# A hybrid decoder layer on one core: the scan's state update moved ahead of its decay products, and the last products cut at 512, 384 and 128 tokens

## The chip, the cores and the metric

The kernel runs on one core of one Trainium2 chip. A core has five engines with a queue of their own each: PE (TensorE, matrix products; its weight loads are listed apart as PEld), DVE (VectorE), ACT (ScalarE), POOL (GpSimd) and SP (SyncE, which here issues most of the transfers). The metric is the device time of one execution in microseconds (us).

## The reference

One layer of a decoder over 1040 positions (16 meta tokens and 1024 real ones) of width 1024. After a norm and one input projection, three groups of heads work side by side: stick-breaking attention, a Mamba-2 state-space scan, and latent attention (MLA). Their outputs go through one projection and are added; then come a norm, a SwiGLU feed-forward layer of width 2816, and a last norm over the features of each token. All is float32. The scan, in blocks of 128 tokens, is what the first edit touches:

```python
seg = Acs[:, :, :, None] - Acs[:, :, None, :]
Ldec = jnp.exp(jnp.where(tri[None, None, :, :, None, None], seg, -jnp.inf))
CB = jnp.einsum('bclgn,bcsgn->bclsg', Cc, Bc)
y_diag = jnp.einsum('bclsgj,bcsgjp->bclgjp', CB[..., None] * Ldec, X)
...
states = jnp.einsum('bclgn,bclgjp->bcgjpn', Bc, X * decay[..., None])
...
def step(carry, inp):
    cd, st = inp
    return carry * cd[..., None, None] + st, carry
...
y_off = jnp.einsum('bclgn,bcgjpn->bclgjp', Cc, prev) * jnp.exp(Acs)[..., None]
return (y_diag + y_off).reshape(b, L, H, P)
```

The second edit touches the end: `h + (silu(fn @ w_gate) * (fn @ w_up)) @ w_down`, then `rmsnorm(h, final_norm_g)`.

## The kernel before

Features lie on the 128 partitions and tokens along the rows, so a product takes a 128x128 piece of a weight as its stationary operand and up to 512 tokens as its moving one. For accuracy each float32 operand is split into a high and a low part, and each product is done as three (high by high, low by high, high by low), which accumulate in one bank of PSUM.

The order of instructions is not written out by hand. The code gives a program order with priorities, and a scheduler with a timeline of its own places each engine's instructions; an engine then runs its own list strictly in that order. So a moved line of code can move many instructions, also of neighbouring stages.

**The scan** (`ssd_chunk`, L764 to L856) runs over nine chunks c (the first holds the 16 meta tokens) and, within a chunk, over two groups g of eight heads; one pair (c, g) is called a half-step here. In a half-step:

- L802: products R spread the running sums of the decay over all partitions, four heads to a bank; ACT makes from them `cd` (the chunk's decay), `ea` (the decay since the chunk's start, one buffer, L811) and, head by head, the exponents of the decay matrices L (L814), then L itself (L824). DVE makes `dec` (L805).
- L820: POOL makes Xd, the inputs times the decay to the chunk's end.
- L826 to L829: product cbp; DVE masks it and multiplies it into L.
- L834, L835: product yo of the state S[g] with C; DVE multiplies it into `ea`.
- L838: eight products yd of the inputs X with L.
- L843, L844: POOL adds `ea` to the output y, then DVE adds yd to it.
- L847 to L854 (not in the last chunk): product sps, POOL multiplies S[g] by cd (L851), DVE adds sps to it (L854). The next chunk's yo of the same g reads S[g].

yo, yd and sps take their banks in turn from one pool of two buffers (`yps`, tag "y"); R has two of its own. While the scan runs, PE also works on dense projections whose rows are L147 to L149 (`dense_fm`: high by high, low by high, high by low): they fill PE between the scan's products.

**The end** (L1600 to L1689). The last products, of the first four of the 22 feed-forward blocks, are done by parts of the tokens. `last_part(t0, n)` does, for each of the eight output blocks o, `down` (12 products of n columns, L1618 to L1620, and DVE's add into the residual hF, L1122), then a square by ACT (L1640). In the first two parts the squares are added up by POOL and DVE, and `token_rstd` sums them over the partitions (L158, one product for each 128 tokens), scales (L169) and takes the power -1/2 on POOL (L170). In the last part (`by_pe`) PE sums each square directly (L1633, one product for each 128 tokens and each o, three blocks late), then DVE scales (L1656) and POOL takes the power (L1657). `last_row` spreads the result over the partitions (L176, one product for each 128 tokens), and `last_norm` copies that row (L1671) and multiplies: some blocks by ACT and POOL (L1676, L1677), the others by DVE (L1679); SP sends each ng finished blocks out (L1681). The row of a part is spread and its norm done while the next part's products run.

```python
r0, _ = last_part(0, 512)
r1, row = last_part(512, 256, between=r0)
last_norm(0, 512, row, (3, 6), 2)
r2, row = last_part(768, 256, True, r1)
last_norm(512, 256, row, range(0, KT, 2), 4)
last_norm(768, 256, last_row(*r2), (1, 4), 2)
```

Of the kernel before, what the change touches and what calls it, by code (L numbers as in the profile page):

```python
# [11 lines left out]
F32 = mybir.dt.float32  # L12
# [47 lines left out]
def tile_hybrid_block(ctx: ExitStack, tc: tile.TileContext, a: dict):  # L60
# [689 lines left out]
    with ExitStack() as st:  # L750
# [13 lines left out]
        def ssd_chunk(c):  # L764
# [26 lines left out]
            for g in range(2):  # L791
# [31 lines left out]
                if c > 0:  # L823
                    act.activation(L, L, AF.Exp, scale=-1.0)  # L824
                    pcb = tp.tile([128, 512], F32, tag="tp", name="cbp")
                    pe.matmul(pcb[:, :128], bc[:, g, :], bc[:, 2 + g, :], start=True, stop=True)  # L826
                    cbm = p2.tile([128, 128], F32, tag="cbm", name="cbm")
                    dve.tensor_tensor(cbm, pcb[:, :128], tri, op=ALU.mult)
                    dve.tensor_tensor(L, L, cbm.unsqueeze(1).to_broadcast([128, 8, 128]), op=ALU.mult)  # L829
                    yo = yps.tile([128, 512], F32, tag="y", name="yo")  # L830
                    yd = yps.tile([128, 512], F32, tag="y", name="yd")
                    for j in range(4):
                        ts = slice(128 * j, 128 * (j + 1))
                        pe.matmul(yo[:, ts], S[g][:, ts], bc[:, 2 + g, :], start=True, stop=True)  # L834
                    dve.tensor_tensor(ea, ea, yo.rearrange("p (j t) -> p j t", j=4), op=ALU.mult)  # L835
                    for h in range(8):
                        hh = 8 * g + h
                        pe.matmul(  # L838
                            yd[64 * (h % 2) : 64 * (h % 2) + 64, 128 * (h // 2) : 128 * (h // 2 + 1)],
                            X[:, hh * 64 : (hh + 1) * 64], L[:, h, :], start=True, stop=True,  # L840
                        )
                    yg = y[:, 4 * g : 4 * g + 4]
                    pool.tensor_tensor(yg, yg, ea, op=ALU.add)  # L843
                    dve.tensor_tensor(yg, yg, yd.rearrange("p (j t) -> p j t", j=4), op=ALU.add)  # L844
                if c < 8:
                    sps = yps.tile([128, 512], F32, tag="y", name="sps")
                    pe.matmul(sps, btok[:n, g * 128 : (g + 1) * 128], Xd[:n, gs], start=True, stop=True)  # L847
                    if c == 0:
                        dve.tensor_copy(S[g], sps)
                    else:  # L850
                        pool.tensor_tensor(  # L851
                            heads(S[g]), heads(S[g]), cd.unsqueeze(2).to_broadcast([128, 8, 64]), op=ALU.mult
                        )
                        dve.tensor_tensor(S[g], S[g], sps, op=ALU.add)  # L854
            if c > 0:
                act.dma_start(s_y[:, :, 128 * (c - 1) : 128 * c].rearrange("j p t -> p j t"), y)  # L856

# [765 lines left out]
    def last_part(t0, n, by_pe=False, between=None):  # L1623

        ts = slice(t0, t0 + n)
        blocks = [(128 * b, 128) for b in range(n // 128)]
        squares, sums = [], []

        def column_sums(o):
            if o == 0:  # L1630
                sums.extend(ffn_bank() for _ in blocks)
            for (b0, w), ps in zip(blocks, sums):
                pe.matmul(ps[:, 0:1], squares[o][:, b0 : b0 + w], ones[:, 0:1], start=(o == 0), stop=(o == KT - 1))  # L1633

        for o in range(KT):
            down(o, t0, n)
            if o == 2 and between:
                row = last_row(*between)
            sq = q_tile("tt")[:, :n]
            act.activation(sq, hT[o][:, ts], AF.Square)  # L1640
            if by_pe:
                squares.append(sq)
                if o >= 3:
                    column_sums(o - 3)
            elif o == 0:
                squares.append(sq)
            else:
                add(squares[0], squares[0], sq, dve if o >= 5 else pool)
        if by_pe:
            for o in range(KT - 3, KT):  # L1650
                column_sums(o)
        with tc.high_priority(offset=1000):
            if sums:
                r = ga.tile([128, len(blocks)], F32, tag="rl", name="rl")
                for e, ps in enumerate(sums):
                    dve.tensor_scalar(r[:, e : e + 1], ps[:, 0:1], 1.0 / D, EPS, ALU.mult, ALU.add)  # L1656
                pool.tensor_tensor(r, r, mhalf[:, : len(blocks)], op=ALU.pow)  # L1657
            else:
                r = token_rstd(ga, bank(), squares, blocks, D)
        return (r, blocks), row if between else None  # L1660
# [21 lines left out]

    rstds = wa.tile([128, 1024], F32, tag="wraw", bufs=1, name="rstds")
    r0, _ = last_part(0, 512)
    r1, row = last_part(512, 256, between=r0)
    last_norm(0, 512, row, (3, 6), 2)
    r2, row = last_part(768, 256, True, r1)
    last_norm(512, 256, row, range(0, KT, 2), 4)
    last_norm(768, 256, last_row(*r2), (1, 4), 2)  # L1689


def _units(w, width=128):
# [85 lines left out]
```

## Time and profile before

| | |
|---|---|
| three timed runs | 1761.19, 1754.87, 1760.85 us (median 1760.85) |
| the profiled execution | 1762.44 us, of which its span is 1760.7 |
| mean granted TensorE clock | 0.986 |
| busy PE / DVE / ACT / POOL | 1706.4 / 1140.2 / 846.2 / 720.0 us |
| moved by DMA | 222.35 MB |

The span runs from the first to the last instruction of the profiled execution. A row of the timeline gives start and length in us, the engine, the line of the code, the operation, output and inputs by the program's names, the shape, how many equal rows are merged (x8), and in brackets the idle time before it with what ended it. A float32 product that is not split is recorded as two rows, so the 8 products yd of a half-step are 16 records. A group's row gives the count, the busy total in us and the mean length of one in ns, then the idle time before them. A row of waits gives who waited for whom, the total in us, the times and the longest. PE's rows overlap: the pace of a stream is the distance from start to start.

### The profile page before, as it was taken

To read this page: it belongs to the slowest core of one execution; us is meant where nothing else is said; L and a number is where in the kernel's file an instruction comes from. 1 tells how busy PE (TensorE), PEld (TensorE's weight loads), DVE (VectorE), ACT (ScalarE), POOL (GpSimd) and SP (SyncE) were. 2 spreads that over 40 slices of the span, in tenths; PEclk is the share of its full clock that TensorE was granted. 3 is DMA by queue.
4 is the path that set the end of the run, shared out by engine and by line. 5 is a ranking of instruction groups with operands and counts; after the bars stand their busy time and mean duration, and the time that the engine had idled before them with its cause. 6 is when DMAs were issued, how large, how long until landed. Compare 5 with 4: busy or idle time off the path is not lost. (4 is left out here: it accounts for less than half of the span.)

```text
span 1760.7 us, 26573 instructions
## 1 busy us (share of the span) xinstructions
PE 1706.4 (97%) x9801; PEld 1500.3 (85%) x9801; DVE 1140.2 (65%) x1742; ACT 846.2 (48%) x1797; POOL 720.0 (41%) x498
## 2 busy tenths in 40 slices
PE   8979999999999899999999999999999999999998
PEld 7969989999987788998888888778888888878887
DVE  7778666678444663555575655986566666688644
ACT  7546565655467646675454425432222232244332
POOL 3334346344466657563321346544455545200012
PEclk9989999999999999999999998999999999999998
DMA  4312232122533645347330443123333223999702
GB/s 162 82 56 64 71 86 79 58 71 73 156 111 115 200 157 154 108 125 244 110 91 29 124 155 102 60 84 101 109 102 102 96 90 104 314 370 386 254 1 97
DMA packets 145639, 222.35 MB, mean 126 GB/s; under 512 B 24722, under 2 KB 84148, under 8 KB 145508
## 3 DMA queue, kind: packets, MB, share of 16 engines
q1 hardware_dynamic: 126112, 205.09, 35.9%
q10 hardware_dynamic: 19396, 15.56, 2.9%
q8 instruction: 77, 1.26, 0.3%
q14 instruction: 54, 0.44, 0.1%
HBM read 157.56 MB, written 63.04 MB: 125 GB/s over the span
## 5 line engine op out<-in xcount | busy, mean ns | idle before, releaser
L147 PE MATMUL d_ps<-hnh,whi 128*128 128x384 f32 (+6 forms) x744 | 250.1, 336 | 7.4 <-DVE KS L610 4.7
L149 PE MATMUL d_ps<-hnl,whi 128*128 128x384 f32 (+6 forms) x744 | 246.7, 332 | 0.0
L148 PE MATMUL d_ps<-hnh,wlo 128*128 128x384 f32 (+6 forms) x744 | 245.8, 330 | 0.0
L136 POOL TENSOR_TENSOR wlo<-wraw,whi 128x1024 fp32r<-128x1024 f32 (+1 forms) x57 | 138.0, 2420 | 222.7 <-ACT whi L134 218.3
L147 PEld LDWEIGHTS d_ps<-hnh,whi 128*128 128x128 f32 (+1 forms) x744 | 141.0, 190 | 12.5 <-issue 6.1
L148 PEld LDWEIGHTS d_ps<-hnh,wlo 128*128 128x128 f32 (+1 forms) x744 | 141.2, 190 | 2.8 <-issue 0.5
L149 PEld LDWEIGHTS d_ps<-hnl,whi 128*128 128x128 f32 (+1 forms) x744 | 140.9, 189 | 2.8 <-issue 0.2
L1285 PE MATMUL b_ps<-T,wl 128*128 128x512 f32 x352 | 138.8, 394 | 1.3 <-POOL wl L1116 1.3
L1286 PE MATMUL b_ps<-T,wh 128*128 128x512 f32 x352 | 138.2, 394 | 1.3 <-DVE T L1116 1.3
L1284 PE MATMUL b_ps<-T,wh 128*128 128x512 f32 x352 | 139.1, 396 | 0.0
L315 DVE TENSOR_TENSOR pl<-ptg,ph 128x512 fp32r<-128x512 f32 (+1 forms) x160 | 99.3, 627 | 48.2 <-ACT ph L314 46.9
L1115 ACT CAST op<-raw 128x1024 fp32r<-128x1024 f32 x69 | 71.3, 1050 | 107.4 <-PE d_ps L1570 59.2
L1116 DVE TENSOR_TENSOR op<-raw,op 128x1024 fp32r<-128x1024 f32 x69 | 84.8, 1239 | 39.0 <-ACT op L1115 38.9
L704 DVE TENSOR_TENSOR_SCAN cm<-cm,zcol 128x144 f32<-128x144 f32 (+3 forms) x64 | 101.7, 1593 | 12.3 <-ACT cm L702 11.9
L314 ACT CAST ph<-ptg 128x512 fp32r<-128x512 f32 (+1 forms) x160 | 85.2, 543 | 39.9 <-PE ptg L331 24.7
L1116 POOL TENSOR_TENSOR wlo<-raw,whi 128x1024 fp32r<-128x1024 f32 x18 | 45.6, 2531 | 110.0 <-ACT whi L1115 110.0
L1116 POOL TENSOR_TENSOR wl<-raw,wh 128x512 fp32r<-128x512 f32 x46 | 74.4, 1625 | 29.2 <-ACT wh L1115 29.2
L1115 ACT CAST wh<-raw 128x512 fp32r<-128x512 f32 x88 | 53.1, 615 | 67.2 <-PE b_ps L1286 67.1
L1122 POOL TENSOR_TENSOR tt<-tt 128x512 f32<-128x512 f32 (+1 forms) x8 | 8.1, 1011 | 186.1 <-ACT tt L1640 185.9
L1012 ACT ACTIVATE pr<-sc_ps,sm 128x256 f32<-128x256 f32 (+4 forms) x112 | 59.8, 540 | 46.8 <-DVE sm L1009 24.8
L1285 PEld LDWEIGHTS b_ps<-T,wl 128*128 128x128 f32 x352 | 66.5, 189 | 16.8 <-POOL wl L1116 1.6
L502 DVE SCALAR_TENSOR_TENSOR cacc<-d_ps,cw,cacc 128x384 f32<-128x384 f32 (+3 forms) x108 | 61.7, 571 | 29.5 <-ACT cacc L495 27.4
(442 smaller groups left out, 5180.8 us busy)
## 6 DMA issues: line engine op xcount, KB each, us to landing
raw<-in_w_down_dram SPq DMA_DIRECT2D x99, 256.0 KB, 5.3
s_hops<-gs SPq DMA_DIRECT2D x63, 256.0 KB, 2.0
raw<-s_hops SPq DMA_DIRECT2D x63, 256.0 KB, 5.4
raw<-in_w_gate_dram SPq DMA_DIRECT2D x22, 512.0 KB, 3.6
raw<-in_w_up_dram SPq DMA_DIRECT2D x22, 512.0 KB, 4.1
wraw<-in_w_o_dram SPq DMA_DIRECT2D x16, 512.0 KB, 4.5
wraw<-in_w_xbc_dram SPq DMA_DIRECT2D x12, 512.0 KB, 3.6
s_xs<-csig SPq DMA_DIRECT2D x24, 192.0 KB, 1.9
```

What stands on the lines that cost most here:

```text
L136: pool.tensor_tensor(lo[:, :cols], raw[:, :cols], f32(hi[:, :cols]), op=ALU.subtract)
L147: pe.matmul(ps[:m, :n], wh, mh, start=(kt == 0), stop=False)
L148: pe.matmul(ps[:m, :n], wl, mh, start=False, stop=False)
L149: pe.matmul(ps[:m, :n], wh, ml, start=False, stop=(kt == nkt - 1))
L314: act.copy(ph[:, :n], pt[:, :n])
L315: dve.tensor_tensor(pl[:, :n], pt[:, :n], f32(ph[:, :n]), op=ALU.subtract)
L704: dve.tensor_tensor_scan(rev, rev, zcol.to_broadcast([128, n_all]), 1.0, ALU.mult, ALU.add)
L1115: act.copy(hi, value)
L1116: eng.tensor_tensor(lo, value, f32(hi), op=ALU.subtract)
L1284: pe.matmul(banks[j], hi[:, ks], UH[u][k], start=start and k == 0, stop=False, skip_group_check=skip)
L1285: pe.matmul(banks[j], lo[:, ks], UH[u][k], start=False, stop=False, skip_group_check=skip)
L1286: pe.matmul(banks[j], hi[:, ks], UL[u][k], start=False, stop=stop and k == 3, skip_group_check=skip)
```

## The change

In a half-step, the state's update (sps, POOL's multiply, DVE's add) stands in the program ahead of the yd products and the two additions to y; yd takes its bank behind sps, no longer behind yo. At the end the parts are 512, 384 and 128 tokens long, no longer 512, 256 and 256; the middle part's outputs go out by two blocks at a time, no longer by four.

```diff
                     yo = yps.tile([128, 512], F32, tag="y", name="yo")
-                    yd = yps.tile([128, 512], F32, tag="y", name="yd")
                     for j in range(4):
...
                     dve.tensor_tensor(ea, ea, yo.rearrange("p (j t) -> p j t", j=4), op=ALU.mult)
-                    for h in range(8):
-                        hh = 8 * g + h
-                        pe.matmul(
-                            yd[64 * (h % 2) : 64 * (h % 2) + 64, 128 * (h // 2) : 128 * (h // 2 + 1)],
-                            X[:, hh * 64 : (hh + 1) * 64], L[:, h, :], start=True, stop=True,
-                        )
-                    yg = y[:, 4 * g : 4 * g + 4]
-                    pool.tensor_tensor(yg, yg, ea, op=ALU.add)
-                    dve.tensor_tensor(yg, yg, yd.rearrange("p (j t) -> p j t", j=4), op=ALU.add)
                 if c < 8:
                     sps = yps.tile([128, 512], F32, tag="y", name="sps")
...
                         dve.tensor_tensor(S[g], S[g], sps, op=ALU.add)
+                if c > 0:
+                    yd = yps.tile([128, 512], F32, tag="y", name="yd")
+                    for h in range(8):
...
+                    yg = y[:, 4 * g : 4 * g + 4]
+                    pool.tensor_tensor(yg, yg, ea, op=ALU.add)
+                    dve.tensor_tensor(yg, yg, yd.rearrange("p (j t) -> p j t", j=4), op=ALU.add)
...
-    r1, row = last_part(512, 256, between=r0)
+    r1, row = last_part(512, 384, between=r0)
     last_norm(0, 512, row, (3, 6), 2)
-    r2, row = last_part(768, 256, True, r1)
-    last_norm(512, 256, row, range(0, KT, 2), 4)
-    last_norm(768, 256, last_row(*r2), (1, 4), 2)
+    r2, row = last_part(896, 128, True, r1)
+    last_norm(512, 384, row, range(0, KT, 2), 2)
+    last_norm(896, 128, last_row(*r2), (1, 4), 2)
```

What the scheduler makes of the first edit is seen on PE around the ninth half-step with yd. Before (xtp and btp are transposes, rows L147 to L149 the dense products between):

```order
L781 MATMUL xtp<-identr,xs 128x128 x4
L789 MATMUL btp<-identr,bc 128x128 x2
L838 MATMUL yd<-L,X 64x128 x8
L847 MATMUL sps<-Xd,btok 128x512
L147 MATMUL d_ps<-lhi,whi 128x272
```

Now (line numbers are one or more higher or lower; sps is L837, yd L849, and the dense rows here are those of the values, L916 to L918):

```order
L918 MATMUL d_ps<-wlo,lhi 128x512
L837 MATMUL sps<-Xd,btok 128x512
L781 MATMUL xtp<-identr,xs 128x128 x4
L789 MATMUL btp<-identr,bc 128x128 x2
L849 MATMUL yd<-L,X 64x128 x8
L916 MATMUL d_ps<-whi,lhi 128x512
```

sps has moved from behind yd to ahead of it, with transposes between, and other dense products surround the half-step. On DVE, in the scan's first third, the additions to the state (S_5503 is group 0's) and to y stood so before:

```order
L844 TENSOR_TENSOR y<-y,yd 128x512
L854 TENSOR_TENSOR S_5503<-S_5503,sps 128x512
L828 TENSOR_TENSOR cbm<-cbp,tri 128x128
L829 TENSOR_TENSOR L<-L,cbm 128x1024
L835 TENSOR_TENSOR ea<-ea,yo 128x512
```

and stand so now (L844 is the addition to the state, L855 that to y, L834 the product into ea):

```order
L844 TENSOR_TENSOR S_5503<-S_5503,sps 128x512
L805 TENSOR_TENSOR dec<-R,AT 128x4
L855 TENSOR_TENSOR y<-y,yd 128x512
L834 TENSOR_TENSOR ea<-ea,yo 128x512
L828 TENSOR_TENSOR cbm<-cbp,tri 128x128
L829 TENSOR_TENSOR L<-L,cbm 128x1024
```

The state's addition has moved ahead of y's, and here the product into ea ahead of that into L. At the end of POOL's list (the hF numbers are the eight output blocks, 15847 to 15854) before:

```order
L170 TENSOR_TENSOR rc<-rc,mhalf 128x2
L1677 TENSOR_TENSOR outt<-hF_15847,rstds 128x256
L1677 TENSOR_TENSOR outt<-hF_15849,rstds 128x256
L1677 TENSOR_TENSOR outt<-hF_15851,rstds 128x256
L1677 TENSOR_TENSOR outt<-hF_15853,rstds 128x256
L1657 TENSOR_TENSOR rl<-rl,mhalf 128x2
L1677 TENSOR_TENSOR outt<-hF_15848,rstds 128x256
L1677 TENSOR_TENSOR outt<-hF_15851,rstds 128x256
```

Now:

```order
L170 TENSOR_TENSOR rc<-rc,mhalf 128x3
L1678 TENSOR_TENSOR outt<-hF_15847,rstds 128x384
L1678 TENSOR_TENSOR outt<-hF_15849,rstds 128x384
L1678 TENSOR_TENSOR outt<-hF_15851,rstds 128x384
L1678 TENSOR_TENSOR outt<-hF_15853,rstds 128x384
L1658 TENSOR_TENSOR rl<-rl,mhalf 128x1
L1678 TENSOR_TENSOR outt<-hF_15848,rstds 128x128
L1678 TENSOR_TENSOR outt<-hF_15851,rstds 128x128
```

The order of the steps is the same; the four norms of the middle part ahead of the last power are wider, what follows it is narrower. All line numbers below are those of the kernel before, unless said otherwise.

More of the change, by code (lines that the diff above doesn't have):

```diff
@@ L854, in ssd_chunk @@
                         dve.tensor_tensor(S[g], S[g], sps, op=ALU.add)
+                if c > 0:
+                    yd = yps.tile([128, 512], F32, tag="y", name="yd")
+                    for h in range(8):
+                        hh = 8 * g + h
+                        pe.matmul(
+                            yd[64 * (h % 2) : 64 * (h % 2) + 64, 128 * (h // 2) : 128 * (h // 2 + 1)],
+                            X[:, hh * 64 : (hh + 1) * 64], L[:, h, :], start=True, stop=True,
+                        )
+                    yg = y[:, 4 * g : 4 * g + 4]
+                    pool.tensor_tensor(yg, yg, ea, op=ALU.add)
+                    dve.tensor_tensor(yg, yg, yd.rearrange("p (j t) -> p j t", j=4), op=ALU.add)
             if c > 0:
```

## The prediction

> **What bounds the kernel now.** I read the page first, then the busy times by stage, then the waits of the scan (the stage of the state-space chunks), then the timeline of the end.
>
> ```profile
> span 1760.7 us, 26573 instructions
> PE 1706.4 (97%) x9801; PEld 1500.3 (85%) x9801; DVE 1140.2 (65%) x1742; ACT 846.2 (48%) x1797; POOL 720.0 (41%) x498
> ```
>
> PE is busy for 1706.4 of 1760.7 us, so all its idle time together is 54.3 us. The stages say where it lies (columns: length, busy of PE, PEld, DVE, ACT, POOL, granted clock, DMA share, GB/s):
>
> ```profile
> 470.00:650.00 180.00, 170.21 (x1233) 143.47 (x1233) 103.53 (x173) 112.26 (x314) 108.74 (x74) 0.98 0.48 150
> 650.00:1100.00 450.00, 440.13 (x2606) 395.59 (x2606) 248.07 (x489) 240.16 (x550) 196.01 (x129) 0.98 0.42 127
> 1722.00:1760.70 38.70, 30.57 (x254) 30.11 (x253) 17.32 (x41) 11.17 (x26) 12.09 (x15) 0.89 0.31 110
> ```
>
> The scan lies in the first row: PE idles 9.8 us there. The last row holds the two parts of 256 tokens; PE is full until the chain after its last product. So the first edit can win at most what PE idles in the scan, and the second acts on PE's own time and on the chain behind it. The idle of the scan, in its two bad places:
>
> ```profile
> 540.00:550.00 10.00, 7.47 (x50) 6.46 (x51) 4.23 (x6) 7.86 (x24) 7.35 (x6) 0.68 0.26 81
> 580.00:620.00 40.00, 34.21 (x256) 28.14 (x254) 28.52 (x45) 24.53 (x68) 24.65 (x16) 1.00 0.60 198
> ```
>
> In the first the granted clock also falls to 0.68. Who waits for whom there (total us, times, longest):
>
> ```profile
> ACT ea L811 <- POOL y L843: 22.3, 9, 4.0
> DVE L L829 <- ACT L L824: 19.6, 12, 4.2
> ...
> PE yd L838 <- DVE L L829: 4.7, 8, 1.2
> ...
> PE R L802 <- ACT L L814: 2.3, 4, 1.4
> ...
> DVE S L854 <- POOL S L851: 1.5, 1, 1.5
> ...
> PE yo L834 <- DVE y L844: 1.4, 1, 1.4
> ```
>
> PE waits at yd for the decay matrices, at R for ACT to empty a bank, and once at yo for the output sum. No row has PE waiting for the state itself. ACT loses 22.3 us at ea, whose only buffer POOL's sum has to release.
>
> **The sum's base.** The profiled execution took 1762.44 us, its span and 1.74 us around it; that is 1.59 us above the median of the runs shown, 1760.85. I add changes to 1762.44 and carry them over to the median.
>
> **Part one, the state's update ahead of yd.** The update is one product (sps), POOL's multiply and DVE's add, with no DMA; the instructions stay the same and their order changes. yo, yd and sps share two PSUM buffers in turn. Before, the next half-step's yo takes the buffer of yd, and so waits for L844 behind the whole L chain: the 1.4 us row. Now it takes that of sps, which L854 empties earlier. That 1.4 us goes. Late next is sps, which takes yd's buffer of the half-step before; it stands a half-step later, so L844 is long done. On DVE L854 now stands ahead of L844 and at times of L829; while it waits (for POOL: 1.5 us once), L829 and with it yd wait behind it.
>
> The waits at yd and R (4.7 and 2.3 us) would shrink only if the L chain came earlier against PE's queue. It might: ACT's L exponentials stand behind ea, and with yo no longer behind L844, ea, POOL's sum and the next ea may come earlier in each half-step. But PE's order was rebuilt with the same belief. By the order, 112 dense products stood between the scan's last yd and the first MLA scores; now it is 184. Thus 72 products have left the scan as cover. At 384 columns,
>
> ```profile
> 651.67 0.34 PE L149 MATMUL d_ps<-hnl,whi 128*128 128x384 f32 x1
> ...
> 654.84 0.34 PE L149 MATMUL d_ps<-hnl,whi 128*128 128x384 f32 x1
> ```
>
> (18 products in 3.17 us, 0.1761 us each), that is 72 x 0.1761 = 12.7 us by which the scan must run faster, or PE idles more. The bounds of part one: -9.8 us (all idle gone), +12.7 us (the cover gone, the pace as it was). I take the 1.4 us that has a mechanism, and 0.5 us (a tenth) of the 4.7: -1.9 us. The reordered rows up to the MLA attention have 9.9 us of idle (second stage row) and no wait that the edit names; I leave them at zero.
>
> **Part two, 512, 384 and 128 tokens.** Each part has 8 x 4 x 3 = 96 products. At 256 columns:
>
> ```profile
> 1722.27 0.28 PE L1618 MATMUL b_ps<-op 128*128 128x256 f32 x1
> ...
> 1727.13 0.27 PE L1620 MATMUL b_ps<-op 128*128 128x256 f32 x1
> ```
>
> 41 steps in 4.86 us, 0.1185 us each; at 384 it is 0.1761. For 128 columns no such stream exists. The nearest rows:
>
> ```profile
> 68.50 0.27 PE L697 MATMUL sc_ps<-KS,Q 128*128 128x144 f32 x1
> ...
> 68.61 0.27 PE L700 MATMUL sc_ps<-sb_mask,identr 128*128 128x128 f32 x1
> ...
> 68.72 0.34 PE L696 MATMUL sc_ps<-K,Q 128*128 128x272 f32 x1
> ```
>
> ```profile
> 636.40 1.09 PE L838 MATMUL yd<-L,X 128*64 128x128 f32 x16
> ```
>
> ```profile
> 1749.38 1.88 PEld L1633 LDWEIGHTS b_ps<-ones,tt 128*128 128x128 f32 x16
> ```
>
> With a load of 128 columns for each, short products follow one another at 0.11 us (68.50, 68.61, 68.72), and bare loads at (1.88 - 0.19) / 15 = 0.113. With loads of 64 columns 128-column products follow at (1.09 - 0.27) / 15 = 0.055. So the weight load, not the columns, sets the pace: 0.11 us, between 0.055 and 0.1185. [...]
>
> PE until its last product: 96 x (0.1761 + 0.11) = 27.5 us against 192 x 0.1185 = 22.8: +4.7. Small products among them: 20 before (sums 4 + 2, spreads 4 + 2, column sums 8), now 18 (4 + 3, 4 + 3, 4), each two records of 0.113: -0.45. So PE's last product ends 4.3 us later. Behind it, before:
>
> ```profile
> 1746.70 0.61 PE L176 MATMUL d_ps<-identr,rc 128*128 128x128 f32 x4
> ...
> 1747.79 2.81 POOL L1677 TENSOR_TENSOR outt<-hF,rstds 128x256 f32<-128x256 f32 x4 [3.33 <-ACT rstds L1671]
> ...
> 1749.38 0.28 PE L1620 MATMUL b_ps<-op 128*128 128x256 f32 x1
> ...
> 1750.16 0.42 ACT L1640 ACTIVATE tt<-hF 128x256 f32<-128x256 f32 x1 [1.14 <-DVE hF L1122]
> 1751.16 0.38 DVE L1656 TENSOR_SCALAR rl<-b_ps 128x1 f32<-128x1 f32 x2 [1.04 <-PE b_ps L1633]
> 1751.62 0.69 POOL L1657 TENSOR_TENSOR rl<-rl,mhalf 128x2 f32<-128x2 f32 x1 [1.02 <-DVE rl L1656]
> ...
> 1752.37 1.23 PE L176 MATMUL d_ps<-identr,rl 128*128 128x128 f32 x4 [1.02 <-POOL rl L1657]
> 1753.63 0.37 ACT L1671 COPY rstds<-d_ps 128x256 f32<-128x256 f32 x1 [3.06 <-PE d_ps L176]
> 1754.03 2.44 DVE L1679 SCALAR_TENSOR_TENSOR outt<-hF,gfin,d_ps 128x256 f32<-128x256 f32 x6 [2.50 <-ACT rstds L1671]
> ```
>
> From 1749.38 to the span's end are 11.32 us. What 128 columns save there, by the slopes between the forms:
>
> ```profile
> L1640 ACT ACTIVATE tt<-hF 128x256 f32<-128x256 f32 x16 | 6.5, 416 | 15.4 <-DVE hF L1122 12.6 <-DVE rc L169 1.5 <-POOL rc L170 1.4
> L1122 DVE TENSOR_TENSOR hF<-hF,b_ps 128x256 f32<-128x256 f32 x16 | 6.5, 418 | 9.4 <-PE b_ps L1620 9.4
> L1640 ACT ACTIVATE tt<-hF 128x512 f32<-128x512 f32 x8 | 5.0, 631 | 15.8 <-DVE hF L1122 15.8
> ...
> L1122 DVE TENSOR_TENSOR hF<-hF,b_ps 128x512 f32<-128x512 f32 x26 | 17.3, 684 | 18.3 <-PE b_ps L1620 11.8 <-PE b_ps L1570 6.5
> ...
> L1679 DVE SCALAR_TENSOR_TENSOR outt<-hF,gfin,d_ps 128x512 f32<-128x512 f32 x6 | 4.0, 742 | 0.2 <-ACT rstds L1671 0.2
> ```
>
> DVE's add 0.42 - 0.13, ACT's square 0.42 - 0.11, two column-sum records fewer (0.22), one L1656 for two (0.2): -0.66. L176 with half its records: -0.5. The copy: -0.1. Six norms from 0.41 us each to 0.26 (slope from 256 to 512: 0.33): -0.9. From the last norm's end (1756.47) to the span's end are 4.2 us, of which one transfer takes 3.0:
>
> ```profile
> out_dram<-outt SPq DMA_DIRECT2D x4, 256.0 KB, 3.0
> ```
>
> Half the bytes, and three transfers of half the size queued ahead of it, I put at -0.9 (none to -1.5). Together -3.1 us: part two costs 4.3 - 3.1 = +1.2 us. POOL is the risk: its four norms of the middle part (0.70 us each at 256, about 1.0 at 384) stand ahead of the last L1657. Before, they began 1.09 us behind their row's spread (1746.70); with two records and a wider copy more that is 1.4. PE's new order has 6 spread records, 4 column-sum records and 26 products from there to its end, 4.0 us, so POOL begins 2.6 us ahead of the last product and is done some 1.5 behind it, just when L1657 becomes ready (2.2 - 0.7): 0 to 0.5, and I take 0. On SP four transfers of 384 KB stand where two of 512 KB stood; the last of them leaves with POOL's fourth norm, over 2 us ahead of the first of the last part. Bounds: with 0.055 us a product -4.1; with 0.1185, no gain in the transfer and POOL late, +3.4.
>
> **The sum.** -1.9 + 1.2 = -0.7: 1761.7 us for a profiled execution, 1760.1 at the median. What a measurement here can tell from no change is about 0.5%, 8.8 us.
>
> **The rivals**, in times at the median.
> - The scan's pace rises everywhere: yd and R find their operands, and the clock holds. For it: ACT's 22.3 us at ea. Against: PE's new order uses that up as 72 products less of cover. It gives -8.4 (1.4 + 4.7 + 2.3), with part two 1753.6, and with all 9.8 us 1752.2.
> - Slower: the scan is bound by ACT, DVE and POOL at the pace it had, and PE, with 12.7 us less cover, waits at yd. It decides from 7.6 of those 12.7 us (8.8 less part two's 1.2). For it: the yd rows, where PE waits already. It gives 1760.85 + 12.7 + 1.2 = 1774.7.
> - The 128-column products run at 0.055: part two -4.1, the sum 1754.9. For it: the 16 yd records. Against: 68.50 to 68.72. [...]
> - The change does little in the scan, since POOL's order had S's multiply directly ahead of the y sum in the first six half-steps already: 0 + 1.2, 1762.1.
>
> **How the numbers follow.** Forecast 0.52, pace 0.15, slower 0.10, fast short products 0.08, nothing in the scan 0.15. Faster by over 0.5% (under 1752.0) needs the pace rival at its end, or it or the short products with the runs' scatter (1754.87 to 1761.19): 0.13. Slower by over 0.5% (over 1769.7): most of its rival and a little scatter, 0.10. Within: 0.77. The range 1752 to 1768 takes in the pace rival and half of the slower one.
>
> **What would show it.** Right: the yo row for L844 gone, yd's wait for L829 between 3 and 7 us, 0.10 to 0.12 us between 128-column products, the last part's PE end about 4.3 us later against its start, 7.7 to 8.7 us from there to the end. Wrong: more than 15 or less than 4 us of PE idle in the scan, 128-column products under 0.09 us, or POOL's L1657 waiting for its norms by over 1 us.

## The result, and the profile after

| | before | changed |
|---|---|---|
| median of 20 runs each | 1759.49 us | 1764.76 us |
| lowest to highest | 1754.87 to 1764.15 | 1760.11 to 1768.79 |
| profiled execution, its span | 1762.44, 1760.7 | 1766.47, 1764.8 |

The ratio is 1.0029, with a 95% interval of 1.0021 to 1.0037: the change costs some 5 us. It lies inside the 0.5% that I called no change, but with 20 runs it is clear of 1, and on the other side of the forecast (1760.1).

The busy times of the changed kernel by stage, the same stretches as before but for the end (columns: length, busy of PE, PEld, DVE, ACT, POOL, granted clock, DMA share, GB/s):

```profile
470.00:650.00 180.00, 172.23 (x1246) 145.36 (x1245) 101.79 (x178) 111.72 (x313) 111.67 (x75) 0.98 0.47 150
650.00:1100.00 450.00, 436.10 (x2603) 391.45 (x2603) 248.70 (x486) 239.38 (x549) 193.54 (x129) 0.98 0.42 126
1722.00:1764.80 42.80, 35.84 (x223) 35.45 (x221) 15.67 (x37) 10.90 (x25) 13.69 (x15) 0.77 0.28 99
```

In the scan PE idles 7.8 us where it idled 9.8. The row to look at is the last: the granted clock of the end has gone from 0.89 to 0.77. The waits of the scan in the changed kernel:

```profile
ACT ea L811 <- POOL y L854: 11.7, 7, 3.7
...
PE d_ps L147 <- ACT lrow L743: 2.7, 1, 2.7
...
PE d_ps L176 <- DVE nope L895: 1.4, 1, 1.4
...
PE d_ps L147 <- DVE rope L946: 1.2, 1, 1.2
...
PE yd L849 <- DVE L L829: 0.9, 2, 0.6
...
PE R L802 <- ACT L L814: 0.4, 1, 0.4
```

ACT's wait at ea is halved (22.3 before), yd's wait for L is 0.9 us (4.7), that of R 0.4 (2.3), and that of yo for L844 is gone. On the other side, products outside the scan's chain (L147 and L176) now wait 2.7, 1.4 and 1.2 us, where the waits of such products came to 1.4 us in all. On balance the scan got better, and more than I forecast. The loss is in the end. Its timeline on PE:

```profile
1719.08 0.34 PE L1619 MATMUL b_ps<-op 128*128 128x384 f32 x1
...
1742.09 0.28 PE L1620 MATMUL b_ps<-op 128*128 128x128 f32 x1
1742.20 0.28 PE L1621 MATMUL b_ps<-op 128*128 128x128 f32 x1
1742.31 0.78 PE L158 MATMUL d_ps<-ones,tt 128*128 128x1 f32 x6
...
1745.22 0.33 PE L1634 MATMUL b_ps<-ones,tt 128*128 128x1 f32 x2
1745.41 0.43 PE L1619 MATMUL b_ps<-op 128*128 128x128 f32 x1
1745.63 0.42 PE L1620 MATMUL b_ps<-op 128*128 128x128 f32 x1
1745.85 0.41 PE L1621 MATMUL b_ps<-op 128*128 128x128 f32 x1
...
1755.02 0.41 PE L1621 MATMUL b_ps<-op 128*128 128x128 f32 x1
1755.23 1.81 PE L1634 MATMUL b_ps<-ones,tt 128*128 128x1 f32 x8
...
1757.32 0.55 POOL L1658 TENSOR_TENSOR rl<-rl,mhalf 128x1 f32<-128x1 f32 x1 [4.34 <-DVE rl L1657]
```

Up to 1745 us the 128-column products follow one another at 0.11 us, as forecast. From 1745.41 on they follow at 0.21 to 0.22, to the end. The clock says why. These are windows of 3.41 us, cut so that one edge falls on the drop:

```profile
1735.22:1738.63 3.41, 3.41 (x25) 3.41 (x24) 2.85 (x6) 1.66 (x4) 0.27 (x1) 1.00 1.01 376
1738.63:1742.05 3.42, 3.42 (x33) 3.42 (x33) 1.99 (x6) 1.38 (x4) 0.00 (x0) 1.00 0.48 179
1742.05:1745.46 3.41, 3.41 (x33) 3.41 (x32) 0.57 (x4) 0.62 (x2) 0.85 (x1) 1.00 0.00 0
1745.46:1748.87 3.41, 3.41 (x18) 3.41 (x17) 0.24 (x1) 1.04 (x3) 0.00 (x0) 0.50 0.02 5
1748.87:1752.29 3.42, 3.42 (x18) 3.42 (x17) 2.39 (x5) 0.46 (x2) 3.20 (x4) 0.50 0.30 108
```

PE is busy for all of each window, and yet the clock goes from 1.00 to 0.50. Half the instructions then fit into a window (18 records instead of 33). In this stretch of the kernel before, the clock fell only behind the last product, at 1751.9.

From the second part's first product (1719.08) to its last one (1755.02) are 35.94 us, to the span's end 45.72. Before, these were 27.11 and 38.43. So the end is 7.3 us longer, where I had put +1.2, and the rest of the profile is 3.2 us earlier, where I had put -1.9.

### The profile page after: what moved, and what is told of

It reads as the page before. It is cut to its first block, busy times and chain, and to the rows that moved or that the text cites. A ratio compares the mean times of both kernels' runs of the same rounds, so it can differ in the third digit from the quotient of the medians.

```text
span 1764.8 us, 26564 instructions
## 1 busy us (share of the span) xinstructions
PE 1709.5 (97%) x9787; PEld 1503.9 (85%) x9787; DVE 1137.3 (64%) x1741; ACT 845.9 (48%) x1797; POOL 722.2 (41%) x498
## 5 line engine op out<-in xcount | busy, mean ns | idle before, releaser
L147 PE MATMUL d_ps<-hnh,whi 128*128 128x384 f32 (+6 forms) x744 | 249.5, 336 | 6.9 <-DVE KS L610 4.7
L149 PE MATMUL d_ps<-hnl,whi 128*128 128x384 f32 (+6 forms) x744 | 245.6, 330 | 0.0
L147 PEld LDWEIGHTS d_ps<-hnh,whi 128*128 128x128 f32 (+1 forms) x744 | 140.5, 189 | 12.2 <-issue 6.5
L149 PEld LDWEIGHTS d_ps<-hnl,whi 128*128 128x128 f32 (+1 forms) x744 | 140.5, 189 | 2.5
L134 ACT CAST whi<-wraw 128x1024 fp32r<-128x1024 f32 (+1 forms) x57 | 59.0, 1034 | 61.4 <-PE d_ps L149 32.9
L1287 PEld LDWEIGHTS b_ps<-T,wh 128*128 128x128 f32 x352 | 66.3, 188 | 16.8 <-DVE T L1117 1.6
```

The costliest lines, as they stand in the source:

```text
L147: pe.matmul(ps[:m, :n], wh, mh, start=(kt == 0), stop=False)
L149: pe.matmul(ps[:m, :n], wh, ml, start=False, stop=(kt == nkt - 1))
L1287: pe.matmul(banks[j], hi[:, ks], UL[u][k], start=False, stop=stop and k == 3, skip_group_check=skip)
```

## The experiments

I started with theory T1: the loss is all in the last parts, where 128-column products leave the array idle for half of the time (my estimate: 0.055 us of each 0.11, by the pace of the yd products) and so bring the clock down, and the scan edit gains. Rivals: R1, the weight loads of the short products make the end longer and the clock has no part in it; R2, the scan edit gives nothing; R3, every stream that runs at the pace of its loads loses the clock. Three more theories (T2, R4 and T3) came up on the way.

A table of ends first, of the profiles on which the argument about the end rests. The times run from the second part's first product, and are read from rows like those above.

| kernel | ratio to before (95% interval) | to the last product | to the end |
|---|---|---|---|
| before | 1 | 27.11 us | 38.43 us |
| changed | 1.0029 (1.0021 to 1.0037) | 35.94 | 45.72 |
| scan edit alone | 0.9975 (0.9962 to 0.9987) | 27.12 | 38.15 |
| parts edit alone | 1.0047 (1.0033 to 1.0061) | 36.41 | 45.80 |
| parts edit, last products 256 wide | 1.0012 (1.0000 to 1.0023) | 32.11 | 40.59 |
| parts 512, 320, 192 | 1.0021 (1.0005 to 1.0037) | 30.56 | 41.95 |
| changed, L158's sums 128 wide | 0.9990 (0.9975 to 1.0005) | 31.38 | 40.56 |
| changed, all last sums 128 wide | 0.9987 (0.9975 to 0.9999) | 31.39 | 40.24 |
| halves side by side | 0.9999 (0.9983 to 1.0014) | 27.64 | 40.47 |
| halves side by side, sums wide | 1.0000 (0.9985 to 1.0015) | 27.65 | 40.36 |
| the same, POOL with two norms | 0.9986 (0.9975 to 0.9998) | 27.65 | 39.92 |

**The two edits apart.** The first kernel takes the changed scan and the old calls at the end:

```diff
-    r1, row = last_part(512, 384, between=r0)
+    r1, row = last_part(512, 256, between=r0)
...
-    r2, row = last_part(896, 128, True, r1)
+    r2, row = last_part(768, 256, True, r1)
```

> The scan edit alone; the last parts stay 512, 256 and 256 tokens. Theory T1 (the whole loss lies in the last parts, where the granted clock halves in the stream of 128-column products, and the scan edit gains): products of the second part start about 3.2 us earlier against the span's start than before, as in the changed kernel, the end stays as before, so 1756.3 us against 1759.5, ratio about 0.998. Rival R2 (the scan edit gives nothing or loses, and the 3.2 us of one profile are scatter): ratio 1.000 or above. Granted clock of the second part 1.00 until its last product, as before, by either.

Measured: 0.9975, 1755.03 us against 1759.04. The scan edit gains 4.4 us (2.3 to 6.7 by the interval). R2 falls. The other kernel has the old scan and the new calls.

> The edit of the last parts alone (512, 384 and 128 tokens); the scan stays as before. T1: the end is 7.3 us longer from the first product of the second part, as in the changed kernel, so about 1767 us, ratio about 1.004 to 1.005; the granted clock falls to 0.50 about 7.7 us into the stream of 128-column products. R2 (the scan edit loses): the ratio is then below the changed kernel's 1.003.

Measured: 1.0047, 1766.90 us, 8.3 us lost. The end is 7.4 us longer, and the clock falls at 1745.86, in the stream of 128-column products. The two ratios add up to 1.0022, within the interval of the change. The loss is the parts edit's alone.

**Is it the clock?** In this kernel the last 128 tokens' products take 128 neighbouring columns along, so the loads stay as they are and the array has twice the work:

```diff
-        hs = slice(t0 % 512, t0 % 512 + n)
+        m = max(n, 256)
+        hs = slice(t0 % 512 + n - m, t0 % 512 + n)
...
-        ps = ffn_bank()[:, :n]
+        ps = ffn_bank()[:, :m]
...
-        add(hT[o][:, ts], hT[o][:, ts], ps)
+        add(hT[o][:, ts], hT[o][:, ts], ps[:, m - n :])
```

> As the parts edit alone, but the products of the last 128 tokens are 256 columns wide: 128 neighbouring columns are computed a second time and not used; the outputs stay the same. The weight loads are the same in number and size, and the array works in more of the time. T1 (the clock falls because 128 columns leave the array idle for about half of each product): the clock stays 1.00 to the last product, products go at 0.1185 us, PE's end is 96 x (0.1761 + 0.1185) = 28.3 us against 22.8, so +5.1 with the small products, the chain behind it about 8 us against 11.3: about +2 us against before, 5 us less than the parts edit alone. Rival R1 (the clock has no part in it; the loads of 128-column products alone make the end longer): 96 x (0.1185 - 0.111) = 0.7 us longer than the parts edit alone.

Measured: 1.0012, 6 us below the parts edit alone, though each product of the last part streams twice the columns. The clock stays at 1.00 to the last product, which comes 5.00 us later than before (forecast 5.1). R1 falls: by it this kernel had to be the slower one. The windows of its last part:

```profile
1735.00:1740.00 5.00, 5.00 (x45) 5.00 (x44) 2.20 (x7) 1.66 (x5) 0.01 (x1) 1.00 0.32 120
1740.00:1747.50 7.50, 7.50 (x66) 7.50 (x65) 3.16 (x8) 2.12 (x6) 3.85 (x5) 1.00 0.15 53
```

**Between the two: 192 columns.**

```diff
-    r1, row = last_part(512, 384, between=r0)
+    r1, row = last_part(512, 320, between=r0)
...
-    r2, row = last_part(896, 128, True, r1)
+    r2, row = last_part(832, 192, True, r1)
```

> The last parts with 512, 320 and 192 tokens; the scan stays as before. 192-column products should still go at the pace of their loads, about 0.113 us, with the array busy in some 0.08 us of each. T1 (the array's busy share decides, with a point somewhere between a half and nine tenths): either clock is possible, and the run tells on which side 0.7 lies. If it holds, PE's end is 96 x (0.147 + 0.113) = 25.0 us against 22.8, +1.8 with the small products, and the chain some 2 us shorter: within 1 us of before. Rival R3 (any stream that goes at the pace of its loads loses the clock): the clock falls to 0.50 some 7.7 us into the stream of 10.9 us, 3 us are lost there and 1.5 behind it: about +4 us.

Measured: 1.0021. In the profiled execution the clock holds until 1744.94, 1.9 us behind the start of the last product, so R3 has a case against it. The end is 3.5 us longer all the same: the products follow at 0.112 us, as forecast, but the last one comes 3.45 us later (forecast 1.8). Part of the difference lies at the column sums, which start 0.22 us behind the product ahead of them (0.11 in the changed kernel); the rest I did not trace. Its 12 times lie between 1756.15 and 1767.15, 11 us apart (8.7 for the changed kernel); whether the clock falls in some executions and holds in others, one profile can't say. This run decides little.

**The short products by themselves.** Everything as before, but the first part's 96 products are cut into 384 of 128 columns:

```diff
-        for e, (w, h) in enumerate(last):
+        step = 128 if n == 512 else n
+        for b in range(0, n, step):
+            for e, (w, h) in enumerate(last):
```

> Everything as before, but the products of the first part (512 tokens) are cut into four of 128 columns each: 384 products instead of 96, with the same results. T1 (128-column products leave the array idle for half of the time and the clock falls some 7 us into such a stream): the clock is 1.00 for 3 to 8 us, then 0.50 for the rest of the stream, with 0.111 us from start to start ahead of the fall and 0.213 behind it: about 7.7 + (384 - 69) x 0.213 = 75 us against 21.9, and it comes back to 1.00 within 7 us of the following products of 256 columns. R1 (the clock falls for another reason at the end of the program, for instance its length or the transfers there): 0.111 us throughout, 42.6 us, clock 1.00.

Measured in a single execution: 1781.88 us, some 24 more. T1 asked for 53 more. The stream's first and last product, with the next part's first behind it, and the clock in the stream's middle:

```profile
1699.38 0.22 PE L1621 MATMUL b_ps<-op 128*128 128x128 f32 x1
...
1742.10 0.28 PE L1623 MATMUL b_ps<-op 128*128 128x128 f32 x1
1742.21 0.34 PE L1621 MATMUL b_ps<-op 128*128 128x256 f32 x1
```

```profile
1708.00:1718.00 10.00, 10.00 (x92) 10.00 (x91) 2.06 (x3) 1.36 (x3) 1.27 (x1) 1.00 0.01 2
1718.00:1728.00 10.00, 10.00 (x92) 10.00 (x91) 1.38 (x2) 2.52 (x4) 2.73 (x3) 1.00 0.00 0
1728.00:1738.00 10.00, 10.00 (x92) 10.00 (x91) 2.07 (x3) 0.86 (x2) 1.10 (x1) 1.00 0.01 2
```

That is 42.8 us for 384 products, 0.111 each. So T1 falls in the form that I gave it, and R3 with it: short products in a row, each at the pace of its load, leave the clock at 1.00 for 42 us. Something else in the changed kernel's last part brings it down.

**What differs, and theory T3.** The first part's stream holds nothing but products. In the changed kernel, the window 1742.05 to 1745.46 also holds the column sums: six records of L158 (the middle part's) and four of L1634 (the last part's own), each with a weight load of 128 columns and a single column behind it. They take about 0.11 us each, as a product of 128 columns does. And the falls are not spread at random. In the profile before, the clock (read in windows of 2 us) falls at 93.0, 110.1, 123.7, 543.6, 680.1, 820.0, 1072.6, 1096.5, 1123.8 and 1751.9 us. All these times are whole multiples of 3.413 us apart ((1751.9 - 93.0) / 486), to within 0.05 us, and the stretches at half clock up to 1127 us are 3.4 or 6.8 us long. In the other profiles it is the same, with another offset in each; a window below is one step of a profile's own grid. One of these falls, at 1096.54, comes with PE as full as in the changed kernel's end, behind seventeen one-column records of L158 and six products of 512 columns:

```profile
1093.13:1096.54 3.41, 3.41 (x25) 3.11 (x25) 3.41 (x4) 3.37 (x6) 1.90 (x2) 1.00 0.00 0
1096.54:1099.95 3.41, 3.41 (x10) 2.64 (x9) 0.43 (x2) 0.74 (x2) 1.01 (x1) 0.50 0.00 0
```

PE was issuing without a gap in the window ahead of this fall, so idle time alone does not tell which windows are followed by one.

What counts may then be how much PE streams: the moving columns of a window's records, counted by their starts. The changed kernel's window ahead of the fall holds 21 products of 128 columns and ten records of one: 2698 columns. In the parts edit alone the window ahead of the fall has 2952. A window of 128-column products alone has 30 or 31 of them, 3840 or 3968 columns, and the clock holds. T3, a guess from these windows: behind one with fewer than about 3000 columns the clock is at a half. At half clock this stream has only 1540 to 2048 columns in a window, and the clock doesn't come back. That the low count is what keeps it down was not tested: elsewhere a window at half clock with 2688 was the last one (from 546.99 in the kernel before), and one with 3584 was not (from 615.65 in the changed kernel).

**The test of T3.** One thing alone is altered in the changed kernel: L158's sums of the last parts' squares stream 128 columns of ones instead of one. The order of all engines' instructions stays the same, and the load sets the pace either way.

```diff
-                    ps[:w, e : e + 1], sq[:, t0 : t0 + w], ones[:, 0:1], start=(i == 0), stop=(i == len(squares) - 1)
+                    ps[:w, k * e : k * (e + 1)], sq[:, t0 : t0 + w], ones[:, 0:k], start=(i == 0), stop=(i == len(squares) - 1)
...
-                r = token_rstd(ga, bank(), squares, blocks, D)
+                r = token_rstd(ga, bank(), squares, blocks, D, k=128)
```

T3 asks for the clock at 1.00 to the last product in most executions. Then 4.8 us ahead of it (half of the 9.6 at half clock) and up to 1.5 behind come back: a ratio of 0.9990 to 1.0005.

> The changed kernel, with one thing altered: the column sums of the first two of the last parts (L158) stream 128 columns of ones instead of one, and only the first column of the result is read; same instructions in the same order, and a record of such a product takes the time of its weight load (0.11 us) either way. [...] Rival T1 (the 128-column products themselves bring the clock down), which the run with the first part by 128 columns already speaks against: ratio about 1.003 again.

Measured: 0.9990 (1757.60 us), 0.4% below the changed kernel, or 7 us, for sums that do 128 times the work. The windows of its last part, and the end of its stream (line numbers are two higher, L1636 for L1634):

```profile
1733.97:1737.38 3.41, 3.41 (x33) 3.41 (x32) 2.40 (x6) 1.79 (x5) 0.00 (x0) 1.00 0.66 246
1737.38:1740.79 3.41, 3.41 (x33) 3.41 (x33) 0.73 (x3) 0.83 (x3) 0.85 (x1) 1.00 0.00 0
1740.79:1744.21 3.42, 3.42 (x33) 3.42 (x32) 0.89 (x3) 1.41 (x4) 0.44 (x1) 1.00 0.03 5
1744.21:1747.62 3.41, 3.30 (x31) 3.22 (x30) 2.27 (x6) 0.71 (x3) 3.41 (x4) 1.00 0.56 202
```

```profile
1738.27 0.88 PE L158 MATMUL d_ps<-ones,tt 128*128 128x128 f32 x6
...
1746.42 0.28 PE L1623 MATMUL b_ps<-op 128*128 128x128 f32 x1
1746.54 1.33 PE L1636 MATMUL b_ps<-ones,tt 128*128 128x1 f32 x8
```

Busy PE and the number of records in a window are as in the changed kernel (33); only the columns differ, and the clock holds to the last product. That one now comes 31.38 us behind the second part's first, 4.6 us earlier than in the changed kernel and 4.27 later than before. Of the 7 us the end accounts for 5.2 in these profiles (45.72 to 40.56); the rest is within the intervals. The window from 1737.38 holds 3714 columns; with the six records counted as one column again it would hold 2952, as many as the one ahead of the fall in the parts edit alone. The windows lie differently in each execution, so the twelve times count for more than the one profile: their interval (0.9975 to 1.0005) lies wholly below the changed kernel's (1.0021 to 1.0037). So the clock's part is shown by an edit of nothing but columns. With the last part's own sums widened too (`ps[:, 0:128]` and `ones` in L1634), T3 asks for 0.9985 to 1.000:

> As the run before it, and the column sums of the last part (L1634) stream 128 columns too. [...] T1: about 1.003.

Measured: 0.9987 (1757.29 us), 31.39 us to the last product, and no fall until 1754.2, behind PE's last instruction. Against the run before it the row's spread of the last part goes at full clock (0.49 us instead of 0.80). One window here has only 2304 columns (1747.36 to 1750.77) and isn't followed by a fall, and in the changed kernel the window from 1090.09 to 1093.50, with 3601 (3089 without a product that starts in its last 0.03 us), is. So the border is not at 3000, or columns are not the whole of the measure: the edit shows that more columns held the clock here, not where a line lies. That stays open.

**The scan: ring or order?** In this kernel only the place where yd takes its bank is undone, so the banks go round as before (yo, yd, sps):

```diff
                     yo = yps.tile([128, 512], F32, tag="y", name="yo")
+                    yd = yps.tile([128, 512], F32, tag="y", name="yd")
...
                 if c > 0:
-                    yd = yps.tile([128, 512], F32, tag="y", name="yd")
                     for h in range(8):
```

> The scan edit alone with one thing undone: yd's bank is taken right behind yo's again (ring yo, yd, sps), while the instructions keep the changed order (state's update ahead of yd); the last parts stay 512, 256 and 256. Theory T2 (my step: the gain comes from the ring, since the next yo no longer takes the bank that the addition of yd to y must empty): the 1.4 us wait of yo is back and the gain of the scan edit alone (ratio 0.9975) falls by more than half, to about 0.999 or above. Rival R4 (the gain comes from the order, which keeps PE from going slack around 540 us, where all four profiles with the old order show the granted clock at a half for 3.4 or 6.8 us and both with the new order show it at 1.00): ratio about 0.9975 again, clock 1.00 from 536 to 556 us.

Measured: 0.9981 (0.9969 to 0.9992). yo's wait of 1.4 us does not come back: no row of this profile has PE waiting at yo. The stage can be measured by itself, from the scan's first R to the first score of the MLA attention. The rows of before, of the scan edit alone and of this kernel:

```profile
478.61 0.35 PE L802 MATMUL R<-A,sel 80*128 80x16 bf16 x8
...
665.66 0.58 PE L997 MATMUL sc_ps<-mhi 96*128 96x144 f32 x3
```

```profile
477.56 0.35 PE L802 MATMUL R<-A,sel 80*128 80x16 bf16 x8
...
660.10 0.58 PE L998 MATMUL sc_ps<-mhi 96*128 96x144 f32 x3
```

```profile
477.99 0.35 PE L802 MATMUL R<-A,sel 80*128 80x16 bf16 x8
...
662.08 0.58 PE L998 MATMUL sc_ps<-mhi 96*128 96x144 f32 x3
```

That is 187.05, 182.54 and 184.09 us. The five profiles with the old scan have 186.7 to 187.7, the eight with the changed one 181.3 to 185.2. So the stage became some 4 us shorter on average (1.9 in the changed kernel's own profile, which has the 185.2), and it is the order that does it, as R4 has it; T2 falls. R4's other half, the clock around 543 us, holds as well. Before (first fence) and with the scan edit alone, in each profile's own windows:

```profile
540.17:543.58 3.41, 1.94 (x18) 1.75 (x19) 1.26 (x2) 3.35 (x12) 2.06 (x3) 1.00 0.27 69
543.58:546.99 3.41, 2.54 (x11) 2.00 (x11) 1.01 (x1) 3.09 (x8) 3.02 (x2) 0.50 0.15 50
546.99:550.41 3.42, 3.24 (x22) 2.66 (x22) 1.85 (x4) 1.72 (x6) 2.10 (x2) 0.50 0.33 115
```

```profile
540.13:543.54 3.41, 3.41 (x40) 3.21 (x40) 2.12 (x6) 3.35 (x12) 0.91 (x1) 1.00 0.00 0
543.54:546.96 3.42, 3.10 (x20) 2.07 (x20) 1.03 (x2) 3.20 (x9) 2.55 (x4) 1.00 0.65 193
```

The same stretch of time holds 40 records of PE instead of 18, and no fall follows. All five profiles with the old order have the clock at half for 6.8 us here, none of the nine with the new order. But six of these nine have a fall at 614 to 616 us, where none of the five has one. In the changed kernel:

```profile
615.65:619.06 3.41, 2.81 (x7) 2.23 (x8) 3.29 (x2) 1.98 (x4) 3.20 (x2) 0.50 0.66 250
```

The stage's length goes with it: 181.3 to 182.5 us in the three profiles without this fall, 182.9 to 183.9 in the three with one window at half clock, 184.1 to 185.2 in the three with two. The changed kernel and the kernel with the ring undone are among the last three, and the latter is the shortest of them. So its 1.5 us more than the scan edit alone go with the clock, and no part for the ring shows.

**Versions that could win.** The next one keeps both edits, and puts the high and the low part of the last 128 tokens' operand side by side, so that each weight is loaded once for 256 columns:

```diff
+            ps = ffn_bank()[:, :256]
+            for e, (w, h) in enumerate(last):
+                wh, wl = (x[:, os] for x in w[o // 4])
+                hb = cmb[:, 256 * e : 256 * (e + 1)]
+                pe.matmul(ps, wh, hb, start=(e == 0), stop=False)
+                pe.matmul(ps, wl, hb, start=False, stop=(e == len(last) - 1))
+            add(hT[o][:, ts], hT[o][:, ts], ps[:, :128])
+            add(hT[o][:, ts], hT[o][:, ts], ps[:, 128:])
```

> The changed kernel (both edits), but in the last 128 tokens the high and the low part of the moving operand lie side by side in one tile, so that each weight operand is loaded once and multiplies 256 columns: 64 products of 256 columns instead of 96 of 128 (low by low, which was left out, is computed too), and DVE adds both halves of the bank. T1 (array busy, clock stays 1.00): the last part's products take 64 x 0.1185 = 7.6 us at full clock; from the first product of the second part to the end 22.75 - 22.75 + 16.9 + 7.6 - 22.75 = +1.3 us of PE's end against before, and 2.7 us less behind it: 37 us against 38.4, and with the scan edit's 4.2 us about 1753.5 us, ratio 0.996 to 0.998; at least 8 us below the changed kernel. R1 (the end is long for other reasons than the 128-column stream, the transfers of the middle part for one): at most 3 us below the changed kernel (the 32 products saved at 0.111).

Measured: 0.9999 (0.9983 to 1.0014), 1757.99 us: some 5 us below the changed kernel by the ratios, and 4 short of the hope. I laid the rest to the column sums and widened them all, and expected 2 to 5 us more from that:

> Both edits, the last 128 tokens with the high and the low part side by side (256 columns), and all the column sums with 128 columns as in the run before. [...]

Measured: 1.0000. That was wrong. Its profile shows another wait. The products are done 3.7 us sooner than with 128 columns, but 12.7 us follow the last one instead of 8.85:

```profile
1743.23 0.83 PE L178 MATMUL d_ps<-identr,rc 128*128 128x128 f32 x6
...
1744.65 3.86 POOL L1693 TENSOR_TENSOR outt<-hF,rstds 128x384 f32<-128x384 f32 x4 [3.63 <-ACT rstds L1687]
...
1748.46 0.55 POOL L1673 TENSOR_TENSOR rl<-rl,mhalf 128x1 f32<-128x1 f32 x1
```

The middle part's row is spread only behind all products (L178 at 1743.23; the last product starts at 1742.89), so the four norms on POOL stand right ahead of the power that the last part needs (DVE had its input at 1745.82). It is the risk that I priced at 0 to 0.5 us for the changed kernel; with a shorter stream ahead of it, it costs 2.6.

```diff
-    last_norm(512, 384, row, range(0, KT, 2), 2)
+    last_norm(512, 384, row, (1, 3), 2)
```

> As the run before it (both edits, halves side by side, wide sums), but POOL does two of the middle part's norms instead of four, and DVE the other six. In that run's profile the last product starts 27.65 us behind the second part's first, 3.7 us earlier than with 96 products of 128 columns, yet 12.7 us follow it instead of 8.9: the middle part's row is spread only behind all products, and POOL's power of the last part (0.55 us) waits for the four norms of 384 tokens (3.85 us). If that is where the gain went: POOL is free 1.9 us earlier, the end comes 1.5 to 2 us earlier against the second part's start, ratio 0.998 to 0.9995, and from the last product to the end about 11 us. If the norms on DVE (six of 0.57 us) or the transfers take its place: no change, ratio 1.000, 12.5 us.

Measured: 0.9986 (0.9975 to 0.9998). POOL's power stands at 1745.41, 3.7 us behind the last product (1741.73) instead of 5.6, but from the last product to the end are still 12.3 us, where I expected 11. The transfers are late next: from 1746 on they are busy without a break,

```profile
1746.00:1748.00 2.00, 0.49 (x2) 0.30 (x2) 1.93 (x7) 0.27 (x1) 0.87 (x2) 0.84 1.02 362
1748.00:1750.00 2.00, 0.00 (x0) 0.00 (x0) 0.47 (x2) 0.00 (x0) 0.00 (x0) 0.50 1.01 350
1750.00:1752.00 2.00, 0.00 (x0) 0.00 (x0) 0.00 (x0) 0.00 (x0) 0.00 (x0) 0.50 0.79 236
```

with the middle part's outputs, which leave as late as the last part's. Last, the scan edit with the old parts, and wide sums in the last parts and ahead of the feed-forward layer:

> The scan edit with the last parts of 512, 256 and 256 tokens, and column sums of 128 columns in the last parts and in the sums ahead of the feed-forward layer (L158, 32 and 26 records in a row about 1069 and 1092 us, where the profiles show the clock at 0.50 for one or two windows). T3: the clock stays 1.00 around 1069 and 1092, two or three windows at half clock go, each worth up to 1.7 us where PE is the bound: 2 to 5 us less than the scan edit alone, ratio to before 0.995 to 0.9965. Rival (PE waits for other engines there anyway, so the half clock costs nothing): 0.9975 again, with the clock at 1.00 there all the same.

Measured: 0.9969 (0.9956 to 0.9982), 1753.39 us. The clock now stays at 1.00 from 1065 to 1080 us (0.89 in the profile of the scan edit alone), but against the scan edit alone (0.9975) the gain can't be told from none. PE idles 0.8 us in this stretch now, where at the lower clock it was full: part of the rival's case, other engines take over. This version and the scan edit alone beat the kernel before, by 5.5 and 4.4 us, and the changed one by some 10.

## Why the prediction was wrong

**The scan: right in sign, too small.** Forecast -1.9, measured -4.4 by the ratio and about 4 us in the stage. The mechanism that I gave the 1.4 us was wrong: the bank ring has little to do with it. The waits at yd and R, of which I took 0.5 us, went almost wholly (4.7 and 2.3 us to 0.9 and 0.4). That the L chain comes earlier fits this (ACT's wait at ea is halved), but was not tested by itself. The two windows at half clock at 543 us went too, though in six of nine profiles one or two came up at 615. The doubt that PE's order had lost 72 products of cover came true in part: the waits of products outside the chain rose from 1.4 to 5.3 us. The rival "does little in the scan" falls, and so does "slower through lost cover". The pace rival had the right waits, but its -8.4 is about twice what was measured, and as a number my -1.9 was nearer.

**The parts: here the prediction failed.** The step is "So the weight load, not the columns, sets the pace: 0.11 us, between 0.055 and 0.1185", used for all 96 products. The pace is right (0.111 measured over 384 of them), but it holds at clock 1.00, and the bounds said nothing of the clock. In the changed kernel it was halved 7.7 us into the stream, and from there on the products came 0.213 us apart. PE's end: forecast +4.3, measured +8.83; with the sums widened +4.27. So the count of products was right, and the clock costs the 4.6 us between. The profile before had shown the clock falling in the slack places, and once, at 1096.54, behind a window in which PE was busy throughout; I read the 0.68 of one of them as a sign of slack, and didn't ask whether the clock could fall in the edit's own stream while PE is full.

**Behind the last product.** Forecast 8.2 us, measured 9.78, of which 0.9 are the half clock (8.85 with all sums wide). The remaining 0.65 is mostly the transfers: from the last norm's end to the span's end are 4.1 us (4.2 before), so the 0.9 that I took for smaller transfers didn't come. That POOL's norms would be done in time was right: L1658 waited for DVE.

**The sum.** -1.9 + 1.2 = -0.7 against about -4.4 + 8.3 by the two edits apart. Without the clock's fall the changed kernel would have been faster by 0.1%, as the runs with wide sums are (0.9990 and 0.9987, the first not clear of 1); the forecast was -0.04%.

## What to carry to other kernels

A stretch in which PE is busy all the time can still lose half its clock (1.00 to 0.50 at 1745.46 here, behind 3.41 us busy of 3.41): look at how many columns its products stream, not only at its idle time, wherever products become short or one-column sums gather. Where such sums go at the pace of their weight loads, a wider moving operand is almost free (0.88 us for six records here, 0.78 with one column), and it held the clock here (the last product 31.38 us behind the second part's first instead of 35.94). And when a stream of products is made shorter, ask which chain of the part before it was hidden there (12.7 us followed the last product here, instead of 8.85).

## What the hardware showed that I had not expected

- The granted clock fell from 1.00 to 0.50 with PE issuing without a gap, behind a window with 2698 columns, and did not come back in the 9.6 us until the last product. With 3840 or 3968 it held for 42 us. No sharp line shows: a window of 3601 was followed by a fall, one of 2304 was not.
- The falls of one execution stand on a grid of 3.413 us with an offset of its own. A stretch of work can so fall into one window or be shared by two, which may be part of why single executions of one kernel differ by 9 us (1754.87 to 1764.15); that link was not tested.
- Six float32 records with a single moving column (0.78 us) and six with 128 columns (0.88 us) take nearly the same time behind loads of 128 columns.
